# The down product of a decoder block as alternating matmuls on two halves of the array's rows

## The chip, the core and the metric

The kernel runs on one core of one Trainium2 chip. The metric is the device time of one execution in microseconds. Two texts are compared: the kernel before, whose time and profile are known here, and the kernel after the change.

## What is computed

The reference is a decoder trunk of two layers on 512 tokens with 1024 features, in float32. Each layer is a feed-forward block, a mixing block (pooling and windowed attention), and another feed-forward block. The change concerns the feed-forward blocks, four in all:

```python
def swiglu(h, w_gu, w_down):
    g, u = jnp.split(h @ w_gu, 2, axis=-1)
    return (jax.nn.silu(g) * u) @ w_down

for l in range(L):
    x = x + 0.5 * swiglu(rmsnorm(x, ln_ffn1[l]), w_ffn1_gu[l], w_ffn1_down[l])
    ...
    x = x + 0.5 * swiglu(rmsnorm(x, ln_ffn2[l]), w_ffn2_gu[l], w_ffn2_down[l])
```

`w_down` is 2816 x 1024, so the hidden vector has 22 blocks of 128 rows and the output has 8 blocks of 128.

## The kernel before

**Numbers.** Every operand of a large product is kept as a rounded high part and the rest, the low part, both in the matmul type fp32r (a 32-bit type of TensorE). A product of two such operands is three matmuls that add into one PSUM bank: high by high, high by low, low by high (`term`, line 297). For the weights the parts are the tiles `wh` and `wl`, made from the loaded tile `raw` by ScalarE (`high`) and VectorE (`low`); for the hidden vector they are `hh` and `hl`.

**Stages.** A feed-forward block (`ffn`, line 447) splits its 22 hidden blocks into three groups, of 6 and 8 and 8 (`groups`; only the very first layer starts with the 6). For each group it computes the gate and up products (`block`, seven smaller products named a11, s2, s1, s3, a12, s4, a22, for each half of the group), multiplies and transposes the result into `hh` and `hl` (`turned`), and then calls `down` (line 617). So there are 4 x 3 = 12 downs.

**A down** has eight outputs, one for each 128 rows of `x`. An output is 8 (or 6) blocks of the hidden vector by three matmuls, each with 128 x 128 weights stationary and 512 tokens moving. The first three outputs are begun with the first half of their blocks, since the second half of the hidden vector is still under way; after the second of them the last transposes are issued (`turn`: eight 128x128 transposes in plain fp32). Then these three are finished, and the other five follow whole. After each output, `done` (line 625) has VectorE compute x = 0.5 * sum + x from the PSUM bank. In the last down of a block it goes on to prepare the operands of the next stage from the new rows of x (`nxt.split`, `nxt.square`); `W.prep` makes the high and low parts of the weights that are needed next and loads more.

**PSUM.** In a feed-forward block the six banks of the pool `pf` go round in turn: `mm()` takes the next one. The gate and up products take six at a time. Two further banks (`pt_tp`, `pt_pv`) serve the transposes.

**Order.** Every engine runs its instructions in the order of the program text (`Engines`, line 98, records each in program order; this is why all rows of the profile name line 95). An instruction waits for others through semaphores only.

**Elsewhere.** The attention scores (`attend`, line 784) are matmuls with 64 rows: head pairs lie on the upper and lower 64 partitions of `qT` and `kT`, and the two halves of a pair write different banks of the tile `sc`. They are plain fp32, of which each matmul appears as two instructions in the trace.

Of the kernel before, what the change touches and what calls it, by code (L numbers as in the profile page):

```python
# [14 lines left out]
ALU = mybir.AluOpType  # L15
# [3 lines left out]
P = 128  # L19
# [3 lines left out]
KT = D // P  # L23
FF = 2816
HT = S // 2
ORDER = ("a11", "s2", "s1", "s3", "a12", "s4", "a22")
FIRST = ("a11", "a12", "s2", "s1", "s3", "s4", "a22")
B11, T1, T2, T3, T4, B21, B22 = range(7)
# [78 lines left out]
def trunk(ctx, tc, xT, consts, vecs, rows, w_g4, w_g3, w_d8, w_d6, w_qkv, w_u, w_pool, w_gate, w_br, w_out, out):  # L107
    nc = Engines(tc)
# [11 lines left out]
    x = xp.tile([P, KT, S], F32, name="x")  # L120
# [17 lines left out]
    def temp(name, dt=F32):  # L138
        return tp.tile([P, S], dt, name=name, tag="t")

    def halves(t):
        return t.rearrange("p (i t) -> p i t", t=HT)

    def split(hi, lo, src, scale=None, between=lambda: None):

        if scale is None:
            nc.scalar.copy(out=hi, in_=src)
            between()
            nc.vector.tensor_tensor(out=lo, in0=src, in1=hi.bitcast(F32), op=ALU.subtract)
        else:  # L150
            nc.scalar.activation(out=hi, in_=src, func=AF.Copy, scale=scale)
            between()
            nc.vector.scalar_tensor_tensor(
                out=lo, in0=src, scalar=scale, in1=hi.bitcast(F32), op0=ALU.mult, op1=ALU.subtract
            )


    class Weights:
# [3 lines left out]
        def __init__(self):  # L162
# [3 lines left out]
            for l in range(L):  # L166
                for f in range(2):
# [8 lines left out]
                    for gi, (at, group) in enumerate(groups(plain)):  # L176
                        for i, n in enumerate(group):
# [5 lines left out]
                            else:  # L183
                                self.block(w, 2 * n, FIRST if 2 * gi + i == int(plain) else ORDER)
                        for m in (HALVES if f == 1 and gi == 2 else range(KT)):
# [109 lines left out]
    W = Weights()  # L295

    def term(pt, i, n, wh, wl, ah, al):
        nc.tensor.matmul(pt, wh, ah, start=i == 0, stop=False)
        nc.tensor.matmul(pt, wh, al, start=False, stop=False)
        nc.tensor.matmul(pt, wl, ah, start=False, stop=i == n - 1)  # L300
# [14 lines left out]
    def mm():  # L315
        return bank["mm"].tile([P, S], F32, name="mm")
# [17 lines left out]
    class Norm:  # L334
# [5 lines left out]
        def split(self, k, between=lambda: None):  # L340

            g = self.gain[:, k:k + 1]
            if self.h is None:
                self.h = xl.tile([P, 7 * 4 * HT], F32R, name="xgh")
                self.l = xl.tile([P, 7 * 4 * HT], F32R, name="xgl")
                self.spare = [t[:, KT * S:] for t in (self.h, self.l)]
# [26 lines left out]
        def first(self, j):  # L373
            d = temp("d")[:, :HT]
            nc.vector.tensor_tensor(out=d, in0=x[:, j, :HT], in1=x[:, j, HT:], op=ALU.subtract)
            split(*self.of(T1, j), halves(d), scale=self.gain[:, j:j + 1])

        def others(self, j, xg, between=lambda: None):
            t, u = temp("t23"), temp("t4")[:, :HT]
            gj = self.gain[:, j:j + 1]  # L380
            nc.vector.scalar_tensor_tensor(
                out=t[:, HT:], in0=x[:, j, HT:], scalar=gj, in1=xg[:, HT:], op0=ALU.mult, op1=ALU.subtract
            )
            nc.vector.scalar_tensor_tensor(
                out=t[:, :HT], in0=x[:, j, :HT], scalar=gj, in1=t[:, HT:], op0=ALU.mult, op1=ALU.subtract
            )
            nc.vector.tensor_tensor(out=u, in0=xg[:, :HT], in1=t[:, :HT], op=ALU.subtract)
            between()
            split(*self.of(T2, j, 2), halves(t))
            split(*self.of(T4, j), halves(u))  # L390
# [56 lines left out]
    def ffn(ctx, nm, nxt, last):  # L447
# [115 lines left out]
        def turn():  # L563
            for t in turns[:2]:
                turned(*t)
            turns[:2] = []
# [50 lines left out]
        def down(hid, kts, final, ms):  # L617
            half = kts // 2

            def part(pd, w, ks):  # L620
                for k in ks:
                    cols = slice(k * P, (k + 1) * P)
                    term(pd, k, kts, w[0][:, cols], w[1][:, cols], hid[0][:, k, :], hid[1][:, k, :])

            def done(m, pd):
                nc.vector.scalar_tensor_tensor(
                    out=x[:, m, :], in0=pd, scalar=0.5, in1=x[:, m, :], op0=ALU.mult, op1=ALU.add
                )
                if final and nxt is not None:
                    nxt.split(m, W.prep)  # L630
                    nxt.square(m)
                    return
                if final and last:
                    nc.sync.dma_start(out=out[m * P:(m + 1) * P, :], in_=x[:, m, :])
                W.prep()

            begun = []
            for i in range(3):
                begun.append((mm(), W.take("dn")))
                part(*begun[-1], range(half))  # L640
                if i == 1:
                    turn()
            for m, b in zip(ms, begun):
                part(*b, range(half, kts))
                done(m, b[0])
            for m in ms[3:]:
                pd = mm()
                part(pd, W.take("dn"), range(kts))
                done(m, pd)

        for gi, (_, group) in enumerate(groups(nm is first)):
            hid = [hp.tile([P, 8, S], F32R, name=n) for n in ("hh", "hl")]
            base = 0
            for i, n in enumerate(group):
                if nm is first and gi == i == 0:
                    plain(n, base, hid)
                else:
                    block(n, base, hid, FIRST if W.sums is None else ORDER)
                base += n // P
            final = gi == 2  # L660
            if final:
                W.sums = None
            down(hid, base, final, HALVES if final and nxt is not None and nxt.halves or final and last else list(range(KT)))
# [284 lines left out]
    for k in range(KT):  # L948
        nc.sync.dma_start(out=x[:, k, :], in_=xT[k * P:(k + 1) * P, :])
        if k < 2:  # L950
            c = W.loads[0]
            cols = slice(k * c["n"] // 2, (k + 1) * c["n"] // 2)
# [88 lines left out]
```

## Time and profile before

| | us |
|---|---|
| median of three runs | 1919.28 (1918.14 to 1919.29) |
| the profiled execution's own time | 1918.39 |
| its span, first to last instruction | 1916.6 |
| TensorE busy in it | 1897.8 |
| VectorE busy in it | 1296.1 |
| ScalarE busy in it | 843.2 |

The profile is of one execution. Engines: PE is TensorE's matmuls, PEld its weight loads, DVE is VectorE, ACT is ScalarE, POOL is GpSimd, SP is the queue that issues loads. A row of a matmul names the tiles as out<-moving,stationary. Matmuls follow each other before the one ahead has ended, so the duration of one says less than the time from start to start, which the timeline gives.

### The profile page before, as it was taken

How to read it: one execution, taken by the hardware profiler on the slowest of the kernel's cores; microseconds unless marked ns; L12 is line 12 of the kernel's file. 1: busy time of each engine (PE TensorE's matmuls, PEld its weight loads, DVE VectorE, ACT ScalarE, POOL GpSimd, SP SyncE). 2: the span in 40 equal slices, each digit the busy share in tenths (PEclk: the TensorE clock that was granted, in tenths of full speed). 3: DMA queues.
4: the chain of work that ended last, by engine and by line, in shares of the span. 5: the costliest groups of instructions: out<-in, count | busy, mean ns of one | idle time of the engine just before them, and what ended most of it. 6: DMA issues, size and time to landing. Idle time of an engine off the chain costs nothing.

```text
span 1916.6 us, 24198 instructions
## 1 busy us (share of the span) xinstructions
PE 1897.8 (99%) x9264; PEld 1611.6 (84%) x9264; DVE 1296.1 (68%) x1897; ACT 843.2 (44%) x1283; POOL 82.5 (4%) x102
## 2 busy tenths in 40 slices
PE   8999999999999999999999999999999999999999
PEld 8988888896788888988888898889877888899887
DVE  6768476566657865758787485865665688657683
ACT  6435254344545542535554253443544455334351
POOL 0000000000000000000010000000000000000000
PEclk9999999999999999999999999999999999999999
DMA  6665564321224654566465466632222247456651
GB/s 202 165 168 163 143 161 135 105 89 63 70 88 121 179 140 119 166 169 174 132 158 164 100 169 169 179 118 94 89 67 77 89 103 219 124 142 165 167 159 44
DMA packets 76628, 256.13 MB, mean 134 GB/s; under 512 B 8640, under 2 KB 8896, under 8 KB 76512
## 3 DMA queue, kind: packets, MB, share of 16 engines
q1 hardware_dynamic: 62928, 209.48, 33.7%
q0 software_dynamic: 13296, 44.71, 13.7%
q8 instruction: 73, 1.20, 0.3%
q14 instruction: 43, 0.35, 0.1%
q10 hardware_dynamic: 288, 0.39, 0.1%
HBM read 252.45 MB, written 2.10 MB: 133 GB/s over the span
## 4 chain that ended last, share of the span: by engine, by line
PE 95%; DVE 2%; ACT 1%; DMA 1%; issue 0%; SPq 0%; DVEq 0%
PE mm L95 89%; PE sc L95 2%; PE pt_pv L95 2%; PE pt_tp L95 2%; ACT s L95 1%; DMA raw<-in_w_g 1%; DVE wl L95 0%; DVE m L95 0%; DVE s L95 0%; DVE ssq L95 0%; ACT wh L95 0%; DVE win L95 0%; DVE nm L95 0%; DVE z L95 0%; ACT qT L95 0%
## 5 line engine op out<-in xcount | busy, mean ns | idle before, releaser
L95 ACT CAST wh<-raw 128x1024 fp32r<-128x1024 f32 (+2 forms) x419 | 414.8, 990 | 491.2 <-PE mm L95 459.1
L95 DVE TENSOR_TENSOR wl<-raw,wh 128x1024 fp32r<-128x1024 f32 (+2 forms) x419 | 480.3, 1147 | 113.9 <-PE mm L95 73.7
L95 PE MATMUL mm<-wh,xgh 128*128 128x512 f32 (+2 forms) x1424 | 524.1, 368 | 3.5 <-ACT wh L95 2.6
L95 PE MATMUL mm<-wl,xgh 128*128 128x512 f32 (+2 forms) x1424 | 521.6, 366 | 0.3
L95 PE MATMUL mm<-wh,xgl 128*128 128x512 f32 (+2 forms) x1424 | 521.6, 366 | 0.0
L95 PEld LDWEIGHTS mm<-wh,xgh 128*128 128x128 f32 x1424 | 268.4, 188 | 38.8 <-ACT wh L95 3.1
L95 PEld LDWEIGHTS mm<-wl,xgh 128*128 128x128 f32 x1424 | 268.6, 189 | 35.3 <-DVE wl L95 0.8
L95 PEld LDWEIGHTS mm<-wh,xgl 128*128 128x128 f32 x1424 | 268.5, 189 | 35.2
L95 PE MATMUL mm<-hh,wh 128*128 128x512 f32 x704 | 276.3, 392 | 0.0
L95 PE MATMUL mm<-hh,wl 128*128 128x512 f32 x704 | 274.3, 390 | 0.0
L95 PE MATMUL mm<-hl,wh 128*128 128x512 f32 x704 | 274.0, 389 | 0.0
L95 DVE SCALAR_TENSOR_TENSOR x<-mm,x 128x512 f32<-128x512 f32 x96 | 66.3, 691 | 199.7 <-PE mm L95 199.7
L95 ACT CAST wh<-sums 128x1024 fp32r<-128x1024 f32 (+1 forms) x92 | 90.9, 988 | 165.9 <-PE mm L95 85.1
L95 PEld LDWEIGHTS mm<-hh,wl 128*128 128x128 f32 x704 | 132.1, 188 | 27.7
L95 PEld LDWEIGHTS mm<-hl,wh 128*128 128x128 f32 x704 | 132.3, 188 | 26.7
L95 PE MATMUL mm<-xgh,wh 128*128 128x512 f32 x384 | 154.7, 403 | 0.0
L95 PEld LDWEIGHTS mm<-hh,wh 128*128 128x128 f32 x704 | 132.2, 188 | 26.6
L95 POOL DMA_DIRECT2D raw<-in_w_g x92 | 79.4, 863 | 1742.2 <-DMA raw<-in_w_g 668.6
L95 PE MATMUL mm<-xgl,wh 128*128 128x512 f32 x384 | 150.5, 392 | 0.0
L95 PE MATMUL mm<-xgh,wl 128*128 128x512 f32 x384 | 150.4, 392 | 0.0
L95 DVE TENSOR_TENSOR wl<-sums,wh 128x1024 fp32r<-128x1024 f32 (+1 forms) x92 | 104.1, 1138 | 13.0 <-PE mm L95 13.0
L95 PEld LDWEIGHTS mm<-xgh,wh 128*128 128x128 f32 x384 | 72.5, 189 | 20.2 <-issue 5.6
(203 smaller groups left out, 1976.1 us busy)
## 6 DMA issues: line engine op xcount, KB each, us to landing
raw<-in_w_g SPq DMA_DIRECT2D x160, 512.0 KB, 4.3
raw<-in_w_g POOLq DMA_DIRECT2D x64, 512.0 KB, 7.5
raw<-in_w_d SPq DMA_DIRECT2D x64, 512.0 KB, 3.5
raw<-in_w_g SPq DMA_DIRECT2D x77, 384.0 KB, 3.5
raw<-in_w_gate SPq DMA_DIRECT2D x32, 512.0 KB, 3.4
raw<-in_w_d SPq DMA_DIRECT2D x32, 384.0 KB, 3.4
raw<-in_w_g POOLq DMA_DIRECT2D x28, 384.0 KB, 5.7
raw<-in_w_br SPq DMA_DIRECT2D x16, 512.0 KB, 3.4
```

What stands on the lines that cost most here:

```text
L95: return lambda *args, **kw: self.tc.keep_in_program_order(call(*args, **kw))
```

## The change

The down product alone changes. Each 128-row matmul becomes two of 64 rows: one with the upper 64 partitions of weights and hidden vector, one with the lower 64, issued one after the other. The upper ones add into one PSUM bank, the lower ones into another, so that an output takes two banks from `mm()`. `done` adds both: two VectorE operations, x = 0.5 * p + x for each.

```diff
+HR = P // 2
...
             def part(pd, w, ks):
                 for k in ks:
                     cols = slice(k * P, (k + 1) * P)
-                    term(pd, k, kts, w[0][:, cols], w[1][:, cols], hid[0][:, k, :], hid[1][:, k, :])
+                    for j, (a, b) in enumerate(((0, 0), (0, 1), (1, 0))):
+                        for r in range(2):
+                            rows = slice(r * HR, (r + 1) * HR)
+                            nc.tensor.matmul(
+                                pd[r], w[a][rows, cols], hid[b][rows, k, :],
+                                start=k == j == 0, stop=k == kts - 1 and j == 2,
+                            )
 
             def done(m, pd):
-                nc.vector.scalar_tensor_tensor(
-                    out=x[:, m, :], in0=pd, scalar=0.5, in1=x[:, m, :], op0=ALU.mult, op1=ALU.add
-                )
+                for p in pd:
+                    nc.vector.scalar_tensor_tensor(
+                        out=x[:, m, :], in0=p, scalar=0.5, in1=x[:, m, :], op0=ALU.mult, op1=ALU.add
+                    )
...
-                begun.append((mm(), W.take("dn")))
+                begun.append(((mm(), mm()), W.take("dn")))
...
-                pd = mm()
+                pd = mm(), mm()
```

On TensorE, in the second down of the program: `pt_pv` is the bank of a transpose, `mm_...` are the banks of outputs, `hh`/`hl` and `wh`/`wl` the parts of the hidden vector and the weights. Before, the end of the second begun output and the transposes that follow:

```order
L95 MATMUL mm_1751<-hh_1118,wh_1674 128x512 [waits Activation_49]
L95 MATMUL mm_1751<-hl_1119,wh_1674 128x512
L95 MATMUL mm_1751<-hh_1118,wl_1694 128x512 [waits DVE_49]
...
L95 MATMUL pt_tp_1764<-cst_82,r0_1466 128x128 [waits DVE_49]
L95 MATMUL pt_tp_1764<-cst_82,r0_1466 128x128 x3
...
L95 MATMUL mm_1778<-hh_1118,wh_1696 128x512 [waits Activation_49]
```

Now, at the same place:

```order
L96 MATMUL mm_1924<-hh_1278,wh_1834 128x512 [waits Activation_49]
L96 MATMUL mm_1925<-hh_1278,wh_1834 128x512
L96 MATMUL mm_1924<-hl_1279,wh_1834 128x512
L96 MATMUL mm_1925<-hl_1279,wh_1834 128x512
L96 MATMUL mm_1924<-hh_1278,wl_1854 128x512 [waits DVE_49]
L96 MATMUL mm_1925<-hh_1278,wl_1854 128x512
...
L96 MATMUL pt_tp_1950<-cst_82,r0_1626 128x128 [waits DVE_49]
L96 MATMUL pt_tp_1950<-cst_82,r0_1626 128x128 x3
...
L96 MATMUL mm_1964<-hh_1278,wh_1856 128x512 [waits Activation_49]
L96 MATMUL mm_1965<-hh_1278,wh_1856 128x512
```

Each matmul became two that write different banks; the transposes on the whole array stand where they stood, in between.

On VectorE, in the last down of layer 0, from the seventh output (`mm_7945` before; `mm_9045` and `mm_9046` now) to the eighth. Before:

```order
L95 SCALAR_TENSOR_TENSOR x_86<-mm_7945,x_86 128x512 [waits PE_49]
L95 TENSOR_TENSOR wl_7972<-raw_7646,wh_7930 128x1024 [waits DMAHW5_49]
L95 SCALAR_TENSOR_TENSOR xgl_7729<-x_86,vec_83,xgh_7728 128x256 [waits Activation_49]
L95 TENSOR_TENSOR d_7977<-x_86 128x256
L95 SCALAR_TENSOR_TENSOR xgl_7729<-d_7977,vec_83,xgh_7728 128x256 [waits Activation_49]
L95 TENSOR_TENSOR ssq_7743<-ssq_7743,sq_7981 128x512 [waits Activation_49]
L95 SCALAR_TENSOR_TENSOR x_86<-mm_7984,x_86 128x512 [waits PE_49]
L95 TENSOR_TENSOR wl_8013<-raw_7799,wh_7974 128x1024 [waits DMAHW0_49]
```

Now:

```order
L96 SCALAR_TENSOR_TENSOR x_86<-mm_9045,x_86 128x512 [waits PE_49]
L96 SCALAR_TENSOR_TENSOR x_86<-mm_9046,x_86 128x512 [waits DVE_49,PE_49]
L96 TENSOR_TENSOR wl_9098<-raw_8590,wh_9030 128x1024 [waits DMAHW5_49]
L96 SCALAR_TENSOR_TENSOR xgl_8725<-x_86,vec_83,xgh_8724 128x256 [waits Activation_49]
L96 TENSOR_TENSOR d_9103<-x_86 128x256
L96 SCALAR_TENSOR_TENSOR xgl_8725<-d_9103,vec_83,xgh_8724 128x256 [waits Activation_49]
L96 TENSOR_TENSOR ssq_8739<-ssq_8739,sq_9107 128x512 [waits Activation_49]
L96 SCALAR_TENSOR_TENSOR x_86<-mm_9110,x_86 128x512 [waits PE_49]
L96 SCALAR_TENSOR_TENSOR x_86<-mm_9111,x_86 128x512 [waits DVE_49,PE_49]
L96 TENSOR_TENSOR wl_9165<-raw_8821,wh_9100 128x1024 [waits DMAHW0_49]
```

One operation is added ahead of each `wl`, and it waits for VectorE's own operation before it.

## Rows read from the trace of the kernel before

**Rows 1.** Page: busy time by engine; granted clock; shares of the chain.
```profile
PE 1897.8 (99%) x9264; PEld 1611.6 (84%) x9264; DVE 1296.1 (68%) x1897; ACT 843.2 (44%) x1283; POOL 82.5 (4%) x102
...
PEclk9999999999999999999999999999999999999999
...
PE 95%; DVE 2%; ACT 1%; DMA 1%; issue 0%; SPq 0%; DVEq 0%
```
**Rows 2.** Page, groups: count, busy us, mean ns, idle us before and its releaser.
```profile
L95 DVE SCALAR_TENSOR_TENSOR x<-mm,x 128x512 f32<-128x512 f32 x96 | 66.3, 691 | 199.7 <-PE mm L95 199.7
...
L95 PE MATMUL mm<-hh,wh 128*128 128x512 f32 x704 | 276.3, 392 | 0.0
```
**Rows 3.** Timeline inside two downs, TensorE: start us, duration us, engine, operation.
```profile
963.73 0.39 PE L95 MATMUL mm<-hh,wl 128*128 128x512 f32 x1
...
966.45 0.39 PE L95 MATMUL mm<-hh,wl 128*128 128x512 f32 x1
...
199.13 0.39 PE L95 MATMUL mm<-hl,wh 128*128 128x512 f32 x1
199.13 0.19 PEld L95 LDWEIGHTS mm<-hh,wl 128*128 128x128 f32 x1
```
**Rows 4.** Timeline, TensorE: first matmul of 24 with 256 columns, and the next one.
```profile
375.54 0.28 PE L95 MATMUL sc<-wh,xgh 128*128 128x256 f32 x1
...
378.41 0.28 PE L95 MATMUL mm<-wh,xgh 128*128 128x256 f32 x1
```
**Rows 5.** Timeline, TensorE: transposes ahead of a down, four to a row.
```profile
191.65 0.60 PE L95 MATMUL pt_tp<-cst,v 128*128 128x128 f32 x4
192.09 0.60 PE L95 MATMUL pt_pv<-cst,v 128*128 128x128 f32 x4
```
**Rows 6.** Timeline, TensorE, attention scores; the last two rows answer narrower stretches.
```profile
443.72 0.39 PE L95 MATMUL mm<-xgh,wl 128*128 128x512 f32 x1
444.04 0.73 PEld L95 LDWEIGHTS sc<-kT,qT 64*128 64x128 f32 x8 [0.35 <-issue]
444.04 1.14 PE L95 MATMUL sc<-kT,qT 64*128 64x256 f32 x8
445.10 0.50 PE L95 MATMUL mm<-xgh,wh 128*128 128x512 f32 x1
...
445.44 0.40 PE L95 MATMUL mm<-xgl,wh 128*128 128x512 f32 x1
...
444.36 0.60 PE L95 MATMUL sc<-kT,qT 64*128 64x256 f32 x4
...
444.79 0.38 PE L95 MATMUL sc<-kT,qT 64*128 64x256 f32 x2
```
**Rows 7.** Timeline, VectorE: one row ahead of a down, then layer 0's last down.
```profile
191.85 0.69 DVE L95 TENSOR_TENSOR r<-mm,r 128x512 f32<-128x512 f32 x1 [0.56 <-PE mm L95]
...
934.23 0.69 DVE L95 SCALAR_TENSOR_TENSOR x<-mm,x 128x512 f32<-128x512 f32 x1 [4.02 <-PE mm L95]
...
939.50 0.48 DVE L95 SCALAR_TENSOR_TENSOR t<-x,vec,xg 128x256 f32<-128x256 f32 x1
940.02 0.49 DVE L95 SCALAR_TENSOR_TENSOR t<-x,vec,t 128x256 f32<-128x256 f32 x1
...
966.87 0.69 DVE L95 SCALAR_TENSOR_TENSOR x<-mm,x 128x512 f32<-128x512 f32 x1 [0.51 <-PE mm L95]
967.48 1.22 DVE L95 TENSOR_TENSOR wl<-raw,wh 128x1024 fp32r<-128x1024 f32 x1
...
972.13 1.22 DVE L95 TENSOR_TENSOR wl<-raw,wh 128x1024 fp32r<-128x1024 f32 x1
...
975.61 2.36 DVE L95 TENSOR_TENSOR wl<-sums,wh 128x1024 fp32r<-128x1024 f32 x2
```
**Rows 8.** Timeline, TensorE: the second product of the block behind that down begins.
```profile
972.11 0.39 PE L95 MATMUL mm<-wh,xgh 128*128 128x512 f32 x1
```
**Rows 9.** Timeline, VectorE: the last output of the kernel.
```profile
1912.92 0.69 DVE L95 SCALAR_TENSOR_TENSOR x<-mm,x 128x512 f32<-128x512 f32 x1 [4.75 <-PE mm L95]
```

## The prediction

> **What bounds the kernel now.** I read the page first: TensorE is busy for 99% of the span, 95% of the chain that ended last is TensorE's, and the clock granted was nine tenths or more of full speed in every slice [rows 1]. Then the group rows: the down product is three groups of 704 matmuls of 128x512, 2112 in all, before which TensorE never sat idle; the first of them stands in [rows 2]. Then the timeline inside a down, which gives the figure that the page hides: the page's mean of one (392 ns) holds its latency, while start to start is 2.72 us for twelve, 226.7 ns each [rows 3]. So the down products are 2112 x 0.2267 = 478.8 us, a quarter of the span, and what one of them costs in steady state is nearly all that matters. The 24 matmuls of 256 columns that read the same kind of operands (fp32r) take 119.6 ns each [rows 4]. The difference, 107 ns for 256 columns, is one column per cycle at 2.4 GHz (the upper of the clock's two levels, the one that the granted clock shows). So 512 columns stream in 213.3 ns, and 226.7 - 213.3 = 13.4 ns of each matmul is a fixed gap. The gap is what a change in the matmuls' form could win, 2112 x 13.4 = 28 us at the very most.
>
> **What row halves cost where the kernel has them already.** The attention scores are plain fp32 matmuls with 64 rows that alternate between the upper and the lower half and write different banks, just as the change will have it. Eight of them (four pairs) lie between two ordinary matmuls [rows 6]. The row of all eight spans 1.14 us, with 0.38 to 0.50 for one, so two run at once. The second pair starts at 444.36 and the fourth at 444.79: 0.215 us for a pair of 256 columns. Plain fp32 runs at two cycles a column: a full-array 128x128 fp32 transpose takes 0.11 us (four in 0.44) [rows 5]. So 256 columns stream in 213.3 ns, and the pair costs 2 ns over that, as one full matmul does. A second half is thus all but free once the array is in this mode.
>
> **Term 1, the pairs.** 2112 matmuls become 2112 pairs; each half streams the same 512 columns. If each half keeps its 13.4 ns gap and both run beside each other, a pair takes 226.7 ns as now. On top come between 0 (in [rows 6] a pair stands no further above its streaming than one matmul) and 2 ns (the second half pays that overhead once more); I take 1 ns, and get +2.1 us (0 to +4.2). Weight loads double in number, but a half's load starts with its partner's: eight loads of 64 rows took 0.73 us with 0.19 for one [rows 6]. A full-array load starts as the matmul before it starts, and is over after 0.19 of 0.227 us [rows 3], so loads stay covered; if they came one after the other (0.38 a pair), a pair could not be under 0.38 us, which [rows 6] contradict.
>
> **Term 2, entering and leaving.** In [rows 6] from the matmul at 443.72 to the one at 445.10 are 1.38 us. Less its own 0.227 and four pairs at 0.215, 0.29 are left; and the next starts 0.34 later, 0.11 more than 0.227. So one visit to the half-row mode costs 0.40 us. A down makes two: the first two outputs' first halves, then (after eight full-array transposes, of `turn`) all the rest. There are 12 downs: 24 x 0.40 = +9.6 us. Below, it is 0 if these waits belong to the scores alone; above, I see none.
>
> **Term 3, VectorE.** Each of 96 outputs gets a second multiply-and-add of 0.69 us [rows 2]. It waits for the first, as both write `x`: VectorE's next independent operation starts 0.61 after such a one (966.87 to 967.48 in [rows 7]), and a waiting one about 0.04 after its predecessor's end (939.50 + 0.48 to 940.02 there), so 0.73 us an output. In eleven downs this is covered: an output takes TensorE 5.4 us (4.1 with six blocks). In the last down of layer 0 it is not, because there VectorE also prepares the next layer's operands. It works from 934.23 without a break for TensorE until 966.36, half a microsecond before the last output needs it [rows 7]. Seven outputs' 0.73 make 5.1 us; it comes to the eighth 4.6 us late, and leaves it 5.3 late. Queued behind are the low weights of the next block's second product, begun at 967.48 and 972.13, and those of its third, at 975.61. TensorE takes the first of these at 972.11 [rows 8]. The second, ready 1.22 after its start at 973.35, is wanted twelve matmuls later, at 974.83; 5.3 later it is 3.8 short, and the third product adds 0.7. Less the half microsecond by which TensorE itself comes later, I take +4.0 us (0 to 5).
>
> Six banks hold three outputs instead of six. The fourth output needs the first's banks, 4.1 to 5.4 us after that one's last matmul, for 1.4 us of VectorE: covered, as long as VectorE is not over 2 us behind. The second output's banks are released by the block's last subtraction at 192.54 [rows 7], long before its first matmul twelve after 192.45: nothing. At the kernel's end the second addition lies bare between the last matmul and the last store: 0.69 [rows 9], +0.7 us.
>
> **Sum.** 1918.39 (the profiled execution's own time, 0.9 under the median of three) + 2.1 + 9.6 + 4.0 + 0.7 = 1934.8 us. With the terms' ends: 1919 to 1938.
>
> **The rivals.** (1) The gap hides behind the other half: faster. Fp32 pairs stand 2 ns over their streaming [rows 6]; if fp32r pairs do too, a pair is 215.5 ns, 11.2 less, 23.7 us in all. VectorE falls 1.9 us further behind in the one down: 1918.4 - 23.7 + 9.6 + 5.9 + 0.7 = 1910.9; it decides from 7 ns a pair, where it has paid for the other terms. For it: the gap is there for fp32r alone, full-array fp32 has only 2 ns. Against: two halves that run in step have their gaps in step, and [rows 3] show the load already beside the matmul. The Trainium skill (TensorE: Matmul & The Clock Gate, Part 3: Packing small matmuls — row/col tiling) says that a weight load overlaps matmuls in flight only where their row groups differ. By that rule alternating halves would win what this rival wins; the trace disagrees for the full array, whose loads start together with the matmul before. (2) Half of it, if the gap goes with the rows: 6.7 ns, -14.1 + 15: 1919, no change. (3) The two gaps come one after the other, since something before the array serves one instruction at a time: +13.4 ns a pair, 28.3 us, 1918.4 + 28.3 + 14.3 = 1961. (4) The halves don't run at once, so the change doesn't do what it says. In [rows 6] two halves together take one column per cycle, which is what a single fp32r stream takes alone; if the way into the array or into PSUM has no more, a pair is 453 ns: 1918.4 + 478.8 + 10 = 2407. The rows don't exclude it. The Trainium skill (the same page, section Measured speedup vs the span model) gives 3.07x for four 32-row tiles of 512 columns, which speaks against it; no run here shows that.
>
> **How the numbers follow.** Forecast 0.50, of which 0.06 lies within 0.2% (about what a measurement of this kernel can tell from no change); rival 1 0.18; rival 2 0.06; rival 3 0.14; rival 4 0.12. So faster 0.18, same 0.12, slower 0.70. The likeliest time is 1935. The range runs from 1907 (rival 1 with most of term 2 gone) to 1964 (rival 3 with the ends of its terms); it leaves out rival 4 and about 0.05 of tails.
>
> **What will show it.** In the middle of a down, pairs of matmuls a few ns apart and 227 to 228 ns from pair to pair (rival 1: 215; rival 2: 220; rival 3: 240; rival 4: 453). At the 24 borders, 0.2 us of extra start-to-start on either side. After the last down of layer 0, matmuls of the next block that wait for VectorE's `wl`, 4 us together. VectorE 66 us busier, ScalarE, GpSimd and the queues unchanged. A pair spacing under 220 ns, or borders that cost nothing, would make the prediction wrong.

## The result: 0.9% slower, and the profile after

The changed kernel takes 1936.33 us (median of four, 1935.49 to 1938.80) against 1919.28 before. The ratio is 1.009 with a 95% interval of 1.0075 to 1.0105. The profiled execution took 1935.97, its span is 1934.1, 17.5 over the span before. The forecast was 1934.8.

The page after, busy time by engine and shares of the chain that ended last, to be read beside [rows 1]:

```profile
PE 1907.2 (99%) x11376; PEld 1609.0 (83%) x11376; DVE 1361.2 (70%) x1993; ACT 843.3 (44%) x1283; POOL 82.5 (4%) x102
...
PE 92%; DVE 5%; ACT 2%; DMA 1%; issue 1%; SPq 0%; DVEq 0%; ACTq 0%
```

There are 2112 more matmuls and as many more weight loads, and TensorE is no less busy. VectorE works 65 us more, as 96 additions of 0.69 should. In the chain VectorE goes from 2% to 5% and ScalarE from 1% to 2%: for some time one of them, and not TensorE, sets the pace.

The steady state answers [rows 3]: the timeline of TensorE in the second down of the program (start us, duration us). The first two rows are twelve pairs apart; behind them come the eight transposes and the down's second entry into the half rows; the last three rows are the down's end.

```profile
195.78 0.39 PE L96 MATMUL mm<-hh,wl 64*128 64x512 f32 x2
...
198.50 0.39 PE L96 MATMUL mm<-hh,wl 64*128 64x512 f32 x2
198.82 0.66 PE L96 MATMUL pt_tp<-cst,r 128*128 128x128 f32 x4
199.31 0.60 PE L96 MATMUL pt_pv<-cst,r 128*128 128x128 f32 x4
199.84 0.50 PE L96 MATMUL mm<-hh,wh 64*128 64x512 f32 x2
200.18 0.40 PE L96 MATMUL mm<-hl,wh 64*128 64x512 f32 x2
...
237.83 0.39 PE L96 MATMUL mm<-hh,wl 64*128 64x512 f32 x2
238.14 0.50 PE L96 MATMUL mm<-wh,xgh 128*128 128x512 f32 x1
238.48 0.40 PE L96 MATMUL mm<-wl,xgh 128*128 128x512 f32 x1
```

Twelve pairs take 2.72 us, 226.7 ns each: to the digit what twelve whole matmuls took in [rows 3]. So the pairs cost nothing and win nothing. The borders cost: the last pair is 0.32 ahead of the first transpose, the second four transposes 0.53 ahead of the first pair, and where the down ends, 0.31 and 0.34 stand where 0.227 would. Behind four transposes the kernel before had its first whole matmul after 0.36 (192.09 in [rows 5] to this row):

```profile
192.45 0.47 PE L95 MATMUL mm<-hh,wh 128*128 128x512 f32 x1
```

The one new wait is behind the last down of layer 0. First VectorE, then ScalarE, then TensorE there (the square bracket is the idle time before a row, and what ended it):

```profile
970.46 1.48 DVE L96 SCALAR_TENSOR_TENSOR x<-mm,x 128x512 f32<-128x512 f32 x2
971.86 1.21 DVE L96 TENSOR_TENSOR wl<-raw,wh 128x1024 fp32r<-128x1024 f32 x1
...
975.52 1.48 DVE L96 SCALAR_TENSOR_TENSOR x<-mm,x 128x512 f32<-128x512 f32 x2
...
977.10 0.72 ACT L96 ACTIVATE xg<-x,vec 128x512 f32<-128x512 f32 x1 [2.22 <-DVE x L96]
...
980.68 1.05 ACT L96 COPY r<-mm 128x512 f32<-128x512 f32 x2
...
970.07 0.39 PE L96 MATMUL mm<-hh,wl 64*128 64x512 f32 x2
...
975.76 0.39 PE L96 MATMUL mm<-wh,xgl 128*128 128x512 f32 x1
981.30 0.80 PE L96 MATMUL mm<-wh,xgh 128*128 128x512 f32 x1 [5.15 <-ACT r L96]
981.89 0.63 PE L96 MATMUL mm<-wl,xgh 128*128 128x512 f32 x1
```

VectorE comes to the eighth output at 975.52, though its last pair started at 970.07; in [rows 7] it came at 966.87, 0.42 after the start at 966.45. ScalarE waits for that output too (`xg`), and behind its share of the preparation stand the copies `r`, which empty the banks of the next block's first product. The second product adds into the same banks. So TensorE, done with the first product at 976.15, stands idle for 5.15 us. And then it runs at half clock. Busy time, granted clock (the number behind the engines) and DMA by stretch:

```profile
975.00:981.30 6.30, 1.15 (x7) 0.61 (x5) 6.12 (x11) 4.17 (x8) 0.00 (x0) 0.80 0.00 0
981.30:985.50 4.20, 4.20 (x10) 3.33 (x11) 4.20 (x5) 1.89 (x3) 0.00 (x0) 0.50 0.15 18
985.50:990.00 4.50, 4.50 (x21) 3.70 (x20) 2.97 (x3) 2.56 (x3) 0.86 (x1) 0.99 0.65 226
```

The clock granted falls in the idle stretch (0.80 on average) and is 0.50 behind it (1.2 GHz, the lower of the two levels). Ten matmuls are issued at that level, some 427 ns apart instead of 227, which costs some 2 us, before it is back.

**Where the 17.5 us are.** I set the start of every TensorE instruction of the one trace beside its twin in the other (a pair counted as one) and noted where the lag grows:

| place | us |
|---|---|
| up to the first down | -0.2 |
| borders of the half-row mode, 23.5 visits (the last has no way out) | +8.5 |
| behind the last down of layer 0: 5.3 wait, 2.2 half clock | +7.5 |
| the two mixing blocks, whose code is the same | -0.3 and +1.2 |
| inside the downs, 2112 pairs | 0.0 |
| from the last pair to the end | +0.8 |

The +1.2 is a stretch at half clock behind an idle time of 3.5 us in the second layer's attention; the kernel before has the same idle time there, and in its profile the clock stayed up. Whether it belongs to the change is open. Of the nine versions traced (the experiments below with them), the six that run both halves show it there and the three others don't; behind the same idle time in the first layer's attention all show it but one, the kernel before among them.

### The profile page after: what moved, and what is told of

Same layout as the page of the kernel before. It is cut to its first block, busy times and chain, and to the rows that moved or that the text cites. A ratio compares the mean times of both kernels' runs of the same rounds, so it can differ in the third digit from the quotient of the medians.

```text
span 1934.1 us, 28673 instructions
## 1 busy us (share of the span) xinstructions
PE 1907.2 (99%) x11376; PEld 1609.0 (83%) x11376; DVE 1361.2 (70%) x1993; ACT 843.3 (44%) x1283; POOL 82.5 (4%) x102
## 4 chain that ended last, share of the span: by engine, by line
PE 92%; DVE 5%; ACT 2%; DMA 1%; issue 1%; SPq 0%; DVEq 0%; ACTq 0%
PE mm L96 86%; PE sc L96 2%; PE pt_tp L96 2%; PE pt_pv L96 2%; DVE wl L96 1%; ACT s L96 1%; DMA raw<-in_w_g 1%; DVE x L96 1%; DVE xgl L96 1%; ACT xgh L96 0%; DVE ssq L96 0%; DVE t L96 0%; ACT wh L96 0%; DVE m L96 0%; DVE s L96 0%
## 5 line engine op out<-in xcount | busy, mean ns | idle before, releaser
L96 PE MATMUL mm<-hh,wh 64*128 64x512 f32 x1408 | 276.9, 390 | 0.0
L96 PE MATMUL mm<-hl,wh 64*128 64x512 f32 x1408 | 274.3, 386 | 0.0
L96 PE MATMUL mm<-hh,wl 64*128 64x512 f32 x1408 | 274.3, 386 | 0.0
L96 DVE SCALAR_TENSOR_TENSOR x<-mm,x 128x512 f32<-128x512 f32 x192 | 132.6, 691 | 151.5 <-PE mm L96 140.0
L96 PEld LDWEIGHTS mm<-hh,wh 64*128 64x128 f32 x1408 | 131.8, 184 | 31.0 <-issue 4.0
L96 PEld LDWEIGHTS mm<-hh,wl 64*128 64x128 f32 x1408 | 131.9, 184 | 27.9
L96 PEld LDWEIGHTS mm<-hl,wh 64*128 64x128 f32 x1408 | 132.0, 184 | 27.0
```

Source lines behind the costliest of these rows:

```text
L96: return lambda *args, **kw: self.tc.keep_in_program_order(call(*args, **kw))
```

## The experiments

Medians are of up to five runs; the kernel before had 1919.1 to 1919.9 beside them. Theory A: the pairs are free, and the loss is borders plus one late VectorE. Theory B: every pair costs some 8 ns more. Theory C: the second additions and the scarcer banks cost a little in each down. B is hard to hold against the pairs' 226.7 ns; the runs test it from outside the trace.

**one_add_l0.** In layer 0's last down alone, the second addition is left out:

```diff
+            alone = final and nxt is not None and nxt.halves
...
-                for p in pd:
+                for p in pd[:1] if alone else pd:
```

> In the last down of layer 0 alone the second addition is left out (the lower halves' sums are computed there and not added, so the result lacks them); all matmuls stay as in the changed kernel. Theory A (pairs cost what whole matmuls cost; the 17 us are 24 visits to the half-row mode of 0.36 us, one late VectorE of 7.5 us in layer 0's last down, of which 5.3 us wait and 2.2 us half clock behind it, and 0.8 us at the end): 1936.3 - 7.5 = 1928.8 us, and no wait of TensorE for ScalarE's copy r behind that down. Rival B (every pair costs 8 ns more): 1936, unchanged. Rival C (the second additions and the scarcer banks cost a little in each of the 12 downs): 1935.

Measured: 1929.52 us, ratio 1.0050 (1.0037 to 1.0063). Eight operations of 0.69 us out of one down bring back 6.8 us. In the trace the next block's second product follows without a break:

```profile
976.49 0.39 PE L96 MATMUL mm<-wl,xgh 128*128 128x512 f32 x1
976.71 0.39 PE L96 MATMUL mm<-wh,xgl 128*128 128x512 f32 x1
976.94 0.39 PE L96 MATMUL mm<-wh,xgh 128*128 128x512 f32 x1
```

The row at 976.94 is the matmul that waited 5.15 us in the changed kernel. B and C fall.

**whole_l0.** In that down alone, whole matmuls, one bank, one addition:

```diff
+                    if alone:
+                        term(pd[0], k, kts, w[0][:, cols], w[1][:, cols], hid[0][:, k, :], hid[1][:, k, :])
+                        continue
...
+                begun.append(((mm(),) if alone else (mm(), mm()), W.take("dn")))
...
+                pd = (mm(),) if alone else (mm(), mm())
```

> In the last down of layer 0 alone the matmuls are whole again, with one bank and one addition an output; the other eleven downs are as in the changed kernel. Theory A: 1936.3 - 7.5 - 2 x 0.36 = 1928.1 us. Rival B (8 ns a pair): 168 pairs and 24 less, 1936.3 - 1.5 = 1934.8. Rival C: 1936.3 - 17/12 = 1934.9.

Measured: 1928.28 us, ratio 1.0047 (1.0034 to 1.0060). Undoing the matmuls as well, in the same down, brings only another 1.2 us, of which two visits are 0.7 and the rest is within what runs differ by. The eleven other downs, with the end of the kernel, keep 9 us of the loss.

**whole_two_banks.** The other part alone: banks and additions of the change, matmuls whole:

```diff
+                    for j, (a, b) in enumerate(((0, 0), (0, 1), (1, 0))):
+                        i = 3 * k + j
+                        nc.tensor.matmul(
+                            pd[i % 2], w[a][:, cols], hid[b][:, k, :], start=i < 2, stop=i >= 3 * kts - 2,
+                        )
```

> All matmuls are whole, on 128 rows, but go in turn to two banks an output, and VectorE adds both: the banks and additions of the change without its half rows. Theory A: 1919.3 + 7.5 + 0.8 = 1927.6 us, start to start 227 ns as before, no extra time at the borders of a down. Rival B: 1919.3 (the pairs are gone), or 1920 with the end. Rival C: 1936, nearly all of the loss.

Measured: 1926.14 us, ratio 1.0035 (1.0021 to 1.0049). The wait and the half clock are there without any half row. TensorE's rows and the stretch behind them:

```profile
970.85 0.39 PE L96 MATMUL mm<-wh,xgl 128*128 128x512 f32 x1
976.42 0.79 PE L96 MATMUL mm<-wh,xgh 128*128 128x512 f32 x1 [5.19 <-ACT r L96]
```
```profile
976.40:980.40 4.00, 3.98 (x9) 3.14 (x10) 4.00 (x5) 1.69 (x3) 0.00 (x0) 0.50 0.09 16
```

The time is 1.5 under theory A's figure. By the same comparison of starts the wait and the half clock are 7.5 us here too, and no border shows a step.

**one_visit.** The half rows begin after the down's transposes; what is begun before them goes as whole matmuls into the first of the two banks:

```diff
+                    if mixed and k < half:
+                        for j, (a, b) in enumerate(((0, 0), (0, 1), (1, 0))):
+                            nc.tensor.matmul(pd[0], w[a][:, cols], hid[b][:, k, :], start=k == j == 0, stop=False)
+                        continue
...
+                            first = k == half and r == 1 if mixed else k == 0
...
-                part(*begun[-1], range(half))
+                part(*begun[-1], range(half), i < 2)
...
```

> The first halves of the first two outputs of each down go as whole matmuls into the first of the two banks; the half rows begin after the down's transposes, so a down enters the half-row mode once and not twice. Theory A: 12 visits less, 1936.3 - 12 x 0.36 = 1932.0 us. Rival B (8 ns a pair): one pair in seven or eight less, 1936.3 - 2.2 = 1934.1, and the borders' 0.17 us stay where they are. Rival C: 1936.

Measured: 1933.58 us, ratio 1.0071 (1.0058 to 1.0084): 2.8 less than the changed kernel where A expected 4.3. The borders did what A says. Ahead of the first output there is none any more, ahead of the third there is:

```profile
192.00 0.60 PE L96 MATMUL pt_pv<-cst,v 128*128 128x128 f32 x4
192.36 0.48 PE L96 MATMUL mm<-hh,wh 128*128 128x512 f32 x1
...
198.34 0.60 PE L96 MATMUL pt_pv<-cst,r 128*128 128x128 f32 x4
198.87 0.50 PE L96 MATMUL mm<-hh,wh 64*128 64x512 f32 x2
199.21 0.39 PE L96 MATMUL mm<-hl,wh 64*128 64x512 f32 x2
```

The lag grows by 0.36 us a down here, by 0.70 in the changed kernel. Of the missing 1.5 us some 0.6 went to the late VectorE (8.1 us by the comparison of starts, where the changed kernel has 7.5). Behind layer 0's last down TensorE now stands 0.84 before the first product (for VectorE's addition, row at 969.36) and 4.31 before the second, together as long as the 5.15 of the changed kernel, but 13 matmuls instead of 10 go at half clock:

```profile
969.36 0.47 PE L96 MATMUL mm<-wh,xgh 128*128 128x512 f32 x1 [0.84 <-DVE x L96]
```

The rest is no more than such runs differ by.

**upper_only.** The lower halves are left out, so a 64-row matmul stands alone:

```diff
-                        for r in range(2):
+                        for r in range(1):
```

> The lower halves are left out everywhere (the down product lacks half of its rows), with one bank and one addition an output; the upper halves stay. Theory A (the second half is free): 227 ns from start to start as with pairs, 24 visits stay, no late VectorE: 1919.3 + 8.5 = 1927.8 us. Rival B (a pair costs 8 ns over one half): 1919.3 or less. If the gap of 13 ns went with the rows of a matmul: 220 ns, 1927.8 - 14 = 1914.

Measured: 1927.51 us, ratio 1.0040 (1.0024 to 1.0055), as A has it. Twelve half matmuls alone take 2.72 us:

```profile
195.15 0.39 PE L96 MATMUL mm<-hh,wl 64*128 64x512 f32 x1
...
197.87 0.39 PE L96 MATMUL mm<-hh,wl 64*128 64x512 f32 x1
...
198.68 0.60 PE L96 MATMUL pt_pv<-cst,r 128*128 128x128 f32 x4
199.21 0.50 PE L96 MATMUL mm<-hh,wh 64*128 64x512 f32 x1
```

So 226.7 ns is the price of one half, of two halves beside each other, and of one whole. The gap of 13.4 ns doesn't go with the rows. The border is the same 0.53 as with pairs: it comes with a 64-row matmul, not with the second half.

**three_by_three.** Per block, the three upper halves are issued before the three lower ones (the loops over `r` and `j` change places). The run was meant to show that the alternation makes the halves run at once.

> Per block of the hidden vector the three upper halves are issued, then the three lower ones, where the changed kernel alternates. Theory A with starts in the order of the program: a lower half can stand beside the third upper one only, six matmuls take four slots of 227 ns where the changed kernel takes three: 1936 + 478.8/3 = 2096 us. If the array takes a later matmul ahead of a waiting one: 1936, unchanged. If only neighbours of one weight and one block run at once: 1936 + 479 = 2415.

Measured: 1936.21 us (two runs), ratio 1.0085 (1.0061 to 1.0110). My figure of 2096 was wrong: the time is that of the changed kernel. On TensorE's program the rows of one block are these (`mm_1898` the upper bank, `mm_1899` the lower one):

```order
L96 MATMUL mm_1898<-hh_1278,wh_1814 128x512
L96 MATMUL mm_1898<-hl_1279,wh_1814 128x512
L96 MATMUL mm_1898<-hh_1278,wl_1832 128x512
L96 MATMUL mm_1899<-hh_1278,wh_1814 128x512
L96 MATMUL mm_1899<-hl_1279,wh_1814 128x512
L96 MATMUL mm_1899<-hh_1278,wl_1832 128x512
```

The trace has them two by two, each upper one with its own lower one, 227 ns from pair to pair:

```profile
200.88 0.40 PE L96 MATMUL mm<-hh,wh 64*128 64x512 f32 x2
201.10 0.40 PE L96 MATMUL mm<-hl,wh 64*128 64x512 f32 x2
201.33 0.40 PE L96 MATMUL mm<-hh,wl 64*128 64x512 f32 x2
```

So a lower half starts ahead of upper ones that stand before it in the program. What is said ahead of the prediction, that every engine runs its instructions in the order of the program text, doesn't hold between the two halves on TensorE.

**by_output.** How far ahead? All upper halves of an output before all its lower ones (the loop over `r` outermost in `part`).

> All upper halves of an output (or of the begun half of one: 9 to 24 matmuls) are issued before its lower halves. Three uppers before three lowers cost nothing (1936.2 us), so the halves don't start in the order of the program. Theory D (each half works through its own matmuls in order, and TensorE looks at least 24 matmuls ahead): 1936, pairs still 227 ns apart. Rival E (it looks only some six or so ahead): of 24 uppers most run alone, as do the lowers behind them, and a down takes up to twice its time: 2100 to 2400 us.

Measured: 2226.77 us (two runs), ratio 1.1601 (1.1567 to 1.1634): rival E. The rows of a begun output in the second down, of twelve uppers and twelve lowers:

```profile
212.15 0.50 PE L96 MATMUL mm<-hh,wh 64*128 64x512 f32 x1
...
213.87 0.39 PE L96 MATMUL mm<-hl,wh 64*128 64x512 f32 x1
214.10 0.39 PE L96 MATMUL mm<-hh,wl 64*128 64x512 f32 x1
214.10 0.61 PE L96 MATMUL mm<-hh,wh 64*128 64x512 f32 x2
214.44 0.50 PE L96 MATMUL mm<-hl,wh 64*128 64x512 f32 x2
214.67 0.49 PE L96 MATMUL mm<-hh,wl 64*128 64x512 f32 x2
214.90 0.39 PE L96 MATMUL mm<-hh,wh 64*128 64x512 f32 x1
...
216.06 0.39 PE L96 MATMUL mm<-hh,wl 64*128 64x512 f32 x1
216.06 0.61 PE L96 MATMUL mm<-hh,wh 64*128 64x512 f32 x2
```

Eight uppers run alone (212.15 to 213.87). Beside the ninth, at 214.10, the first lower starts, and three more beside the tenth to twelfth. The fifth to eighth lower are alone; beside the last four, from 216.06 on, start the first four uppers of the next output. The half that is free is given a matmul that stands three places behind the next one in turn, not one farther off.

The halves that run beside each other here are not in step: rows of two last 0.50 where a pair in step has 0.39, so their starts lie 0.11 us apart. Each half still takes some 0.23 us from start to start (214.44, 214.67, 214.90).

## Why the prediction was right

The time, the sign and the mechanism hold: the pairs bring nothing, the borders and one late VectorE cost. Of the four terms three were mis-sized (by -2.1, -1.1 and +3.5 us), and that these errors nearly cancel, so that the sum came within 2 us, is luck.

**Term 1, the pairs** (+2.1, 0 to +4.2): 0.0. A pair is 226.7 ns, the lower end. The row of [rows 6] that had a pair no further above its streaming than one matmul was the right price, and the nanosecond on top had no row behind it. Rival 1 (the gap hides), rival 2 (half of it) and rival 3 (the gaps one after the other) fall with it, and rival 4 too: halves of one column per cycle each do run at once. The argument against rival 1, that halves in step have their gaps in step, agrees with the three equal figures of upper_only, the pairs and the whole matmuls; but by_output's halves, 0.11 us out of step, hide no gap either, so being in step is not the reason. The rule that rival 1 leaned on, from the Trainium skill (TensorE: Matmul & The Clock Gate, Part 3: Packing small matmuls — row/col tiling), that loads overlap matmuls in flight only where row groups differ, finds no support here: differing row groups won not one nanosecond.

**Term 2, the borders** (+9.6): +8.5, or 0.36 a visit where the scores gave 0.40; one_visit shows that they go when the visits go. That the scores' borders were plain fp32 between fp32r made little difference.

**Term 3, VectorE** (+4.0, 0 to 5): +7.5, above the upper end. The place was right, and so was VectorE's lag: the eighth output was reached 5.0 us late (975.52 against 970.07 + 0.42) where the working had 4.6 (an output's extra was 0.79, not 0.73, since 970.46 to 971.86 is 1.40 for what was 0.61). What failed is the step after that. I followed VectorE's own queue, to the low weights, and found them 3.8 us short. I left out that ScalarE waits for the same output, and what is queued behind that on ScalarE: the copies `r`, without which the second product cannot begin at all. Before the change the first of these was done at 971.82, only 0.3 us before the second product at 972.11 [rows 8]:

```profile
971.25 0.57 ACT L95 COPY r<-mm 128x512 f32<-128x512 f32 x1
```

So nearly the whole lag fell on TensorE: 5.3 us. The second omission is the clock: a TensorE idle for 5 us paid 2.2 us more at 1.2 GHz. The prediction spoke of 4 us of waits and didn't ask what follows a wait.

**The banks** (nothing): nothing in the changed kernel's downs; whole_two_banks has no other step than the one place. In one_visit one wait of 0.84 us for an addition shows that the reserve was thin.

**The end** (+0.7): +0.8. The two additions take 1.49 us (row at 1929.57) where one took 0.69 in [rows 9]:

```profile
1929.57 1.49 DVE L96 SCALAR_TENSOR_TENSOR x<-mm,x 128x512 f32<-128x512 f32 x2 [3.95 <-PE mm L96]
```

No version with half rows beats the kernel before: without the one wait, 9 us of borders and end stay, and nothing stands against them.

## What to carry to other kernels

Splitting a full contraction into row halves won nothing here: both halves stream the same columns and keep the same gap, so a whole matmul, one half and two halves all take 226.7 ns from start to start, and the mode has a price at its borders (0.36 us a visit here). Where an engine off the critical path falls behind, follow every engine that waits for its result and what is queued behind that wait, not only its own queue; and add what the clock takes after an idle stretch of some microseconds. An extra operation of 0.7 us an output was free in ten downs, cost 0.8 us at the end of the last one, and 7.5 us in one other: ask for the one stage where the reserve is gone.

## What the runs showed of the hardware

The two row halves each take their matmuls in order, as far as the names in the rows tell, but not in one order with each other: three lower halves issued behind three upper ones started beside them. Of twelve issued in a row only the last four ran beside the first four of the other half. I had expected starts in the order of the program.

The 13.4 ns gap of an fp32r matmul is absent at the lower clock. From 981.89 to 985.30 (eight steps, from the second to the last row at half clock) is 3.41 us, 426 ns each, which is 512 columns at 1.2 GHz with nothing over; plain fp32, at two cycles a column, has 2 ns (0.215 us for 256 columns in [rows 6]):

```profile
981.89 0.63 PE L96 MATMUL mm<-wl,xgh 128*128 128x512 f32 x1
...
985.30 0.53 PE L96 MATMUL mm<-wh,xgh 128*128 128x512 f32 x1
```

In these rows the gap shows only where columns go by at 2.4 a nanosecond, and it is as long for 64 rows as for 128. That would fit a limit in what feeds the array and not in the array; no run here separates the two, and it stays open.
